# Convolution taps that read the matmul result from PSUM, one tap moved to GpSimd

## The chip, the cores and the metric

The kernel runs on one core of a Trainium2 chip. The metric is device time in microseconds of the whole program, as the median of several executions. Before the change three executions took 3285.49, 3292.46 and 3293.97 us, a median of 3292.46 us. One more execution was recorded by the hardware profiler; the quoted rows come from it.

## The reference, cut to what matters

One layer works on 2048 latent tokens of 1024 channels (a 32 x 64 grid) and 256 context tokens: a mixer (a Fourier branch and a gated recurrence), then a gated MLP with a 3x3 depthwise convolution. The change touches only the MLP:

```python
def conv_ffn(h, w_up, conv_w, conv_b, w_down, rows, cols):
    b, l, _ = h.shape
    z = (h @ w_up).reshape(b, rows, cols, 2 * D_FF)            # 1024 -> 5632 channels
    z = lax.conv_general_dilated(z, conv_w[:, :, None, :], window_strides=(1, 1), padding='SAME',
                                 dimension_numbers=('NHWC', 'HWIO', 'NHWC'),
                                 feature_group_count=2 * D_FF)  # nine taps per channel
    z = z.reshape(b, l, 2 * D_FF) + conv_b
    return (jax.nn.silu(z[..., :D_FF]) * z[..., D_FF:]) @ w_down
```

All data is float32. Channels lie on the 128 partitions, so 5632 channels are 44 tiles of 128 channels x 2048 tokens, and the convolution of a tile is nine shifted multiply-adds with one weight per partition.

## The kernel before, in words

Every large product is made of three matmuls on operands that are split into a high part (a cast on ScalarE, line 102) and a remainder (a subtraction, line 103, on GpSimd unless VectorE is named). Phases 1 and 2 make the mixer's output and the normed input h2 of the MLP. They stay as they are.

`phase3` loops over 22 channel pairs j, and for each over two halves: half 0 is the channel tile that goes through silu, half 1 the one that multiplies it. I count the 44 tiles in the order of work, t = 2j + half. For a tile, 96 matmuls (4 blocks of 512 tokens x 8 x 3, lines 144 to 146) fill `z`, four PSUM banks. There are two such buffers, `za` for half 0 and `zb` for half 1, so TensorE fills one while the other is emptied. ScalarE then copies `z` to SBUF (`zs`, line 952, two buffers), makes the centre tap with the bias (`ac`, line 953, three buffers), and VectorE adds the eight other taps from `zs` (line 979). After half 1, `gate` takes silu of the first half on ScalarE (963), multiplies the halves on GpSimd (964) and stores the product to DRAM (`dZ`, 965). The weights `w_up` of a tile have two buffers, so those of tile t+2 are loaded, cast and subtracted once tile t's matmuls are through.

`down` multiplies the stored product with `ffn_down` in eight groups of 22 k-steps, 12 matmuls each (lines 1020 to 1022), into four banks `dn`, two sets in turn. Its first group (gi = 0) loads the weights `wd` too, subtracts most of them on VectorE, and its PSUM pool comes after both `z` buffers are released. Its last input, the product of the last pair, is made by `last()` in the middle of that group.

Each engine works through its own queue in order; the layer that records the program orders each queue, and an instruction that waits holds all that stand behind it on that engine. DMAs are issued from the queue of SyncE.

Of the kernel before, what the change touches and what calls it, by code (L numbers as in the profile page):

```python
# [17 lines left out]
F32 = mybir.dt.float32  # L18
# [8 lines left out]
P = 128  # L27
# [3 lines left out]
NB = 4            # 512-token blocks  # L31
TB = 512
KD = D // P       # 8
DFF = 2816
NF = DFF // P     # 22
# [10 lines left out]
def constants():  # L46
    """Arrays that depend on the shapes alone."""
    n2 = np.arange(128)
    # level masks: entry (s, t) belongs to the level whose block size first separates s and t
# [5 lines left out]
    cmask = np.stack(lev, 1)                       # [s, 8, t]  # L55
    # twiddled 128-point transforms, one table for each residue k1
# [13 lines left out]
    ch = np.stack([np.cos(ang), np.sin(ang)], 1) / 512.0             # [c, 2, c']  # L70
    eye = np.eye(128)
    rst = np.zeros((128, 640))
    rst[:, 127::128] = 1.0                                           # where the scans restart
# [5 lines left out]
def fap(t, off, dims):  # L79
    """Access pattern over the free elements of a whole tile."""  # L80
    a = t[:]
    return bass.AP(a.tensor, a.offset + off, [list(a.ap[0])] + [list(q) for q in dims])


class Banks:
    """PSUM tiles from the pool that holds their tag."""
# [8 lines left out]
class Layer:  # L95
# [3 lines left out]
    # ------------------------------------------------------------------ helpers  # L99
    def split(self, hi, lo, raw, eng=None):  # L100
        """hi = raw rounded to 12 bits, lo = raw - hi."""
        self.nc.scalar.copy(hi, raw)  # L102
        (eng or self.nc.gpsimd).tensor_tensor(lo, raw, hi, op=SUB)  # L103

    def load_split(self, hi, lo, src, eng=None, pool=None, bufs=2):
        """Load [128, n] or [128, k, c] float32 data of at most 512 columns and split it."""
# [10 lines left out]
    def rsqrt(self, pool, v, n):  # L117
        """v ** -0.5 for positive v of shape [128, n]: bit-level guess and three Newton steps."""
# [11 lines left out]
    def load_w(self, ap, name):  # L130
        """A [1024, 128] column tile of a weight matrix -> hi, lo tiles [128, 8, 128]."""
# [8 lines left out]
    def mm3(self, ps, pairs, start=True, stop=True):  # L140
        """Accumulate the products of the (lhs_hi, lhs_lo, rhs_hi, rhs_lo) in pairs."""
# [7 lines left out]
    # ------------------------------------------------------------------ the layer  # L149
# [44 lines left out]
    # ------------------------------------------------------------------ phase 1  # L194
    def phase1(self):
# [6 lines left out]
        self.mod_A = pc.tile([P, KD], F32, name="mod_A")       # norm1_g * (1 + scale)  # L202
# [17 lines left out]
        # the projections fill TensorE between the small products of the two branches  # L220
# [21 lines left out]
    def drain(self):  # L242
        """Trace the rest of the filler's first part and go on to the next."""
        for _ in self.filler.pop(0):
            pass

    def project_all(self, h):
        """The projections of head h for the state passes; from the second head on, with parts of the
        later modulations."""
# [8 lines left out]
    def vec_rows(self, p0):  # L258
        """Small vectors, loaded as rows of 128 and turned into columns."""
# [17 lines left out]
    def startup(self, p0):  # L277
        nc, a = self.nc, self.a
        ps = self.ps
        # silu(c), silu(c_ctx) as columns  # L280
# [7 lines left out]
        # weights of the FNet channels; one half sits where the context goes later  # L288
# [9 lines left out]

        # shift and scale of the first sub-layer, for latents and context: silu(c)^T @ ada_w; the last
        # 512 columns by VectorE, the others by TensorE  # L300
# [45 lines left out]
        # token tiles -> modulated, transposed, split; the products of a block follow the transposes of  # L346
        # the next one
# [24 lines left out]
        # softmax over the two rows of hg_lb, first row  # L372
# [14 lines left out]
        # conv taps as columns  # L387
# [10 lines left out]
    def load_x(self, p0, blk):  # L398
        """The token tiles of a block, each token scaled to unit mean square."""
# [19 lines left out]
    def modulate_steps(self, pool, xs, A, B, hi, lo, tags, every):  # L419
        """[tok, d] tiles -> transposed h = x * A[d] + B[d], split into hi and lo [d, 8, tok]."""  # L420
# [23 lines left out]
    def fill(self, n):  # L444
        """Trace up to n steps of the projections that wait in self.filler; a context in which
        TensorE's instructions are queued behind them."""
# [5 lines left out]
    def project_steps(self, kind, h):  # L452
        """One 128-channel tile of x @ w_in (channel-major), with its activation, to DRAM, in steps
        of three products."""
# [29 lines left out]
    # ------------------------------------------------------------------ FNet branch  # L484
# [9 lines left out]
    def fnet(self, p1, g):  # L494
        nc, a, ps = self.nc, self.a, self.ps
        X = p1.tile([P, 2, TB], F32, name="fX", tag="fX")           # blocks 0, 1 (later G0, G2)
# [436 lines left out]
    def phase3(self, p5):  # L933
        tc, nc, a = self.tc, self.nc, self.a
        with ExitStack() as es:
            es.push(self.psA.__exit__)
            for j in range(NF):
# [19 lines left out]
                if j < NF - 1:  # L957
                    last()
# [119 lines left out]
```

## Time and profile before

| | us |
|---|---|
| median of three executions | 3292.46 |
| lowest, highest | 3285.49, 3293.97 |
| span of the profiled execution | 3293.7 |
| TensorE busy in it | 3128.3 (95%) |
| VectorE busy | 2007.5 (61%) |
| ScalarE busy | 933.0 (28%) |
| GpSimd busy | 957.0 (29%) |

The profiled execution lies 1.2 us over the median of the others, so sums can be made against its span. In the rows, PE is TensorE, DVE VectorE, ACT ScalarE, POOL GpSimd and SP SyncE; "L979" is line 979. Busy time of TensorE is the sum of pipelined matmuls that overlap: one lasts 0.39 us and the next starts after some 0.23 us. Whether TensorE is held up is therefore read from the starts of matmuls and from their number in a stretch of time, not from its busy share.

### The profile page before, as it was taken

Reading aid. Unit: us, or ns where it says so; the run is one execution under the profiler, and the core shown is the slowest. Engines: PE = TensorE matmul, PEld = TensorE weight load, DVE = VectorE, ACT = ScalarE, POOL = GpSimd, SP = SyncE. Lnnn points to the kernel's source line nnn. Section 1 sums busy time; section 2 is a strip of 40 time slices with the busy share of each in tenths; the row PEclk is TensorE's granted clock in tenths of the full one; section 3 lists DMA queues with packets and bytes.
Section 4 is the critical chain, followed back from the end, with each engine's and each line's share of the span. In section 5 each row is a group of like instructions: output and inputs, shape, how many; then the busy total and the mean of one; then the engine's idle time right before and its main releaser. Section 6 shows DMA issues by size and latency. Waiting matters only on the chain.

```text
span 3293.7 us, 38879 instructions
## 1 busy us (share of the span) xinstructions
PE 3128.3 (95%) x14955; PEld 2576.7 (78%) x14955; DVE 2007.5 (61%) x2538; ACT 933.0 (28%) x1498; POOL 957.0 (29%) x514
## 2 busy tenths in 40 slices
PE   7999999999999999999999999999999997999998
PEld 4977788888888888777778777777777776788886
DVE  5355543576666611566458988988988999302324
ACT  3322112233333321333232222222122122323322
POOL 2200110000000011345333434334343343544443
PEclk8999999999999999999999999999999998999999
DMA  6255654423323234555531111101111112534643
GB/s 223 85 166 182 196 166 138 134 95 102 106 90 105 86 111 145 187 165 183 178 110 36 58 36 52 48 32 51 45 36 48 45 46 72 192 121 155 220 147 131
DMA packets 278506, 372.59 MB, mean 113 GB/s; under 512 B 20253, under 2 KB 154289, under 8 KB 274993
## 3 DMA queue, kind: packets, MB, share of 16 engines
q1 hardware_dynamic: 278321, 370.11, 34.3%
q8 instruction: 118, 1.93, 0.2%
q14 instruction: 67, 0.55, 0.1%
HBM read 268.58 MB, written 101.45 MB: 112 GB/s over the span
## 4 chain that ended last, share of the span: by engine, by line
PE 49%; DVE 31%; DMA 8%; issue 5%; ACT 3%; POOL 3%; SPq 0%; ACTq 0%; DVEq 0%; POOLq 0%
DVE ac L979 27%; PE pj L145 8%; PE pj L144 8%; PE pj L146 8%; PE dn L1022 4%; PE dn L1020 4%; PE dn L1021 4%; PE pa L773 3%; ACT ac L953 1%; DMA rw<-in_w_out_dram 1%; DMA rw<-in_w_b_dram 1%; POOL wab L103 1%; PE wo L906 1%; PE wo L908 1%; PE wo L907 1%
## 5 line engine op out<-in xcount | busy, mean ns | idle before, releaser
L979 DVE SCALAR_TENSOR_TENSOR ac<-zs,cw,ac 128x1953 f32<-128x1953 f32 (+2 forms) x352 | 970.2, 2761 | 105.9 <-ACT ac L953 95.3
L146 PE MATMUL z<-h,w_up 128*128 128x512 f32 x1408 | 565.3, 402 | 58.4 <-POOL w_up L103 58.4
L144 PE MATMUL z<-h,w_up 128*128 128x512 f32 x1408 | 560.9, 398 | 1.9 <-DVE mt L912 1.9
L145 PE MATMUL z<-h,w_up 128*128 128x512 f32 x1408 | 560.2, 398 | 0.0
L146 PEld LDWEIGHTS z<-h,w_up 128*128 128x128 f32 x1408 | 272.1, 193 | 126.1 <-POOL w_up L103 69.3
L103 POOL TENSOR_TENSOR w_up<-rw,w_up 128x512 fp32r<-128x512 f32 x88 | 267.5, 3058 | 348.6 <-ACT w_up L102 348.5
L103 POOL TENSOR_TENSOR gl<-rw,gh 128x512 fp32r<-128x512 f32 x176 | 244.4, 1391 | 272.3 <-ACT gh L102 266.0
L144 PEld LDWEIGHTS z<-h,w_up 128*128 128x128 f32 x1408 | 272.6, 194 | 59.2 <-issue 2.3
L145 PEld LDWEIGHTS z<-h,w_up 128*128 128x128 f32 x1408 | 272.0, 193 | 58.4
L1020 PE MATMUL dn<-wd,gh 128*128 128x512 f32 x704 | 278.7, 396 | 22.0 <-ACT zs L952 20.9
L1022 PE MATMUL dn<-wd,gl 128*128 128x512 f32 x704 | 278.9, 396 | 4.0 <-POOL gl L103 4.0
L1021 PE MATMUL dn<-wd,gh 128*128 128x512 f32 x704 | 278.1, 395 | 0.0
L964 POOL TENSOR_TENSOR ac<-ac 128x2048 f32<-128x2048 f32 x21 | 138.8, 6609 | 274.8 <-DVE ac L979 274.8
L102 ACT CAST gh<-rw 128x512 fp32r<-128x512 f32 x176 | 109.1, 621 | 350.9 <-PE dn L1021 219.4
L952 ACT COPY zs<-z 128x2048 f32<-128x2048 f32 x44 | 82.3, 1872 | 392.2 <-PE z L146 392.2
L479 ACT ACTIVATE ev<-pj 128x512 f32<-128x512 f32 (+1 forms) x136 | 79.8, 587 | 354.0 <-PE pj L146 326.3
L1020 PEld LDWEIGHTS dn<-wd,gh 128*128 128x128 f32 x704 | 133.1, 189 | 54.0 <-ACT zs L952 21.3
L1038 DVE TENSOR_TENSOR dtmp<-dn,m 128x512 f32<-128x512 f32 x32 | 21.6, 685 | 247.2 <-PE dn L1022 247.1
L1022 PEld LDWEIGHTS dn<-wd,gl 128*128 128x128 f32 x704 | 133.0, 189 | 38.2 <-POOL gl L103 7.7
L1021 PEld LDWEIGHTS dn<-wd,gh 128*128 128x128 f32 x704 | 133.0, 189 | 30.5
L773 PEld LDWEIGHTS pa<-bQ,bkc 128*128 128x128 f32 x896 | 120.7, 191 | 16.8 <-issue 10.4
L773 PE MATMUL pa<-bQ,bkc 128*128 128x128 f32 x896 | 127.5, 286 | 1.2
(303 smaller groups left out, 6105.8 us busy)
## 6 DMA issues: line engine op xcount, KB each, us to landing
rw<-dZ SPq DMA_DIRECT2D x176, 256.0 KB, 3.1
rw<-in_ffn_up_dram SPq DMA_DIRECT2D x88, 256.0 KB, 3.0
dZ<-ac SPq DMA_DIRECT2D x22, 1024.0 KB, 3.9
rw<-in_w_in_dram SPq DMA_DIRECT2D x80, 256.0 KB, 3.2
maw<-in_ada_w_dram SPq DMA_DIRECT2D x64, 256.0 KB, 3.2
rw<-in_w_out_dram SPq DMA_DIRECT2D x64, 256.0 KB, 2.7
x<-dX SPq DMA_DIRECT2D x48, 256.0 KB, 5.3
rw<-in_ffn_down_dram SPq DMA_DIRECT2D x44, 256.0 KB, 3.1
```

The lines of the kernel that those rows point to most:

```text
L102: self.nc.scalar.copy(hi, raw)
L103: (eng or self.nc.gpsimd).tensor_tensor(lo, raw, hi, op=SUB)
L144: self.nc.tensor.matmul(ps, lh, rh, start=start and i == 0, stop=False)
L145: self.nc.tensor.matmul(ps, lh, rl, start=False, stop=False)
L146: mm = self.nc.tensor.matmul(ps, ll, rh, start=False, stop=stop and i == last)
L773: mm = nc.tensor.matmul(pa[:, c], kc[:, c], fap(Q, w * P, [(2 * m, nw), (W + m, 2), (1, m)]), start=True, stop=True)
L952: nc.scalar.copy(zs, z)
L964: (nc.gpsimd if j < NF - 1 else nc.vector).tensor_tensor(acc[0], acc[0], acc[1], op=MUL)
L979: nc.vector.scalar_tensor_tensor(o, z3[:, r0 + dy:r1 + dy, c0 + dx:c1 + dx], self.cw[:, k, jj:jj + 1], o, op0=MUL, op1=ADD)
L1020: nc.tensor.matmul(accs[i], gh[:, t], wh, start=(kk == 0), stop=False)
L1021: nc.tensor.matmul(accs[i], gh[:, t], wl, start=False, stop=False)
L1022: nc.tensor.matmul(accs[i], gl[:, t], wh, start=False, stop=(kk == NF - 1))
```

## The change

The copy `zs` is gone. ScalarE reads `z` from PSUM twice: for the centre tap `ac`, and for `be`, z times the weight of the tap one row below (tap 7: row +1, column 0). VectorE adds the seven other taps straight from PSUM. GpSimd then adds `be`, shifted by one row of 64, to `ac`. silu of the first half moves ahead of the second half's convolution. The buffers `za` and `zb` stay open into `down`, whose first two groups accumulate in them; and in the first group the remainders of the first eight `wd` tiles are made on GpSimd. (Comments and docstrings are dropped in the new file, which moves no instruction.)

```diff
 def phase3(self, p5):
...
-                    zs = p5.tile([P, SEQ], F32, name="zs", tag="zs", bufs=2)
-                    nc.scalar.copy(zs, z)
-                    nc.scalar.activation(ac, zs, AF.Identity, scale=self.cw[:, 4, jj:jj + 1], bias=self.v("cb", jj))
-                    self.conv(ac, zs, jj)
+                nc.scalar.activation(ac, z, AF.Identity, scale=self.cw[:, 4, jj:jj + 1], bias=self.v("cb", jj))
+                be = p5.tile([P, SEQ], F32, name="be", tag="be", bufs=2)
+                nc.scalar.activation(be, z, AF.Copy, scale=self.cw[:, 7, jj:jj + 1])
+                if half:
+                    nc.scalar.activation(acc[0], acc[0], AF.Silu)
+                self.conv(ac, z, jj)
+                nc.gpsimd.tensor_tensor(ac[:, :SEQ - 64], ac[:, :SEQ - 64], be[:, 64:], op=ADD)
...
 def gate(self, j, acc):
-        nc.scalar.activation(acc[0], acc[0], AF.Silu)
         (nc.gpsimd if j < NF - 1 else nc.vector).tensor_tensor(acc[0], acc[0], acc[1], op=MUL)
         nc.sync.dma_start(self.dZ[j], acc[0])
...
 def conv(self, ac, z, jj):
-                if dy == 0 and dx == 0:
+                if dx == 0 and dy >= 0:
                     continue
...
 def down(self, last, pools):
-                accs = [ps.tile([P, TB], F32, name=f"dn{i}", tag=f"dn{i}_{gi % 2}") for i in range(4)]
+                if gi < 2:
+                    dn = (self.zb if gi else self.za).tile([P, SEQ], F32, name="dn", tag="z")
+                    accs = [dn[:, i * TB:(i + 1) * TB] for i in range(4)]
+                else:
+                    if gi < 4:
+                        (self.psB if gi % 2 else self.psA).__exit__(None, None, None)
+                        ps.append(es.enter_context(tc.tile_pool(name=f"ps3{gi}", bufs=1, reuse_waits="tile", space=PSUM,
+                                                                side="left" if gi % 2 else "right")))
+                    accs = [ps[gi % 2].tile([P, TB], F32, name=f"dn{i}", tag=f"dn{i}") for i in range(4)]
...
-                                        None if gi == 0 and k in (0, 2, 4) else nc.vector, *((self.pw, 2) if gi == 0 else (p6, 4)))
+                                        None if gi == 0 and k < 8 else nc.vector, *((self.pw, 2) if gi == 0 else (p6, 4)))
```

The recording layer moves instructions with it. First place: ScalarE's queue in the middle of phase 3, one pair of tiles. Before (`w_up_...` are the casts of one tile's weights):

```order
L952 COPY zs<-z 128x2048
L102 CAST w_up_16136<-rw 128x512
L953 ACTIVATE ac<-zs,vt,cw 128x2048
L102 CAST w_up_16136<-rw 128x512
L952 COPY zs<-z 128x2048
L963 ACTIVATE ac<-ac 128x2048
L953 ACTIVATE ac<-zs,vt,cw 128x2048
L102 CAST w_up_16254<-rw 128x512 x2
```

and now:

```order
L953 ACTIVATE ac<-z,vt,cw 128x2048
L955 ACTIVATE be<-z,cw 128x2048
L102 CAST w_up_16136<-rw 128x512 x2
L953 ACTIVATE ac<-z,vt,cw 128x2048
L955 ACTIVATE be<-z,cw 128x2048
L957 ACTIVATE ac<-ac 128x2048
L102 CAST w_up_16254<-rw 128x512 x2
```

Before, the silu of a finished pair (L963) stood ahead of the next centre tap (L953), which the next tile's taps need. Now silu (L957) stands behind both reads of `z`. The first tap of a tile waits for both of these reads, since all three read the same banks.

Second place: GpSimd's queue at the same pair. Before (L964 is the gate's product):

```order
L964 TENSOR_TENSOR ac<-ac 128x2048
L103 TENSOR_TENSOR w_up_16136<-rw,w_up_16136 128x512 x2
L103 TENSOR_TENSOR w_up_16254<-rw,w_up_16254 128x512 x2
L964 TENSOR_TENSOR ac<-ac 128x2048
L103 TENSOR_TENSOR w_up_16375<-rw,w_up_16375 128x512 x2
```

and now:

```order
L968 TENSOR_TENSOR ac<-ac 128x2048
L103 TENSOR_TENSOR w_up_16136<-rw,w_up_16136 128x512 x2
L959 TENSOR_TENSOR ac<-ac,be 128x1984
L103 TENSOR_TENSOR w_up_16254<-rw,w_up_16254 128x512 x2
L959 TENSOR_TENSOR ac<-ac,be 128x1984
L968 TENSOR_TENSOR ac<-ac 128x2048
L103 TENSOR_TENSOR w_up_16375<-rw,w_up_16375 128x512 x2
```

Each tile has one addition more (L959), which waits for the tile's seventh tap and holds up the remainders of the weights behind it.

Third place: ScalarE's queue where phase 3 gives way to `down`. Before:

```order
L952 COPY zs<-z 128x2048
L953 ACTIVATE ac<-zs,vt,cw 128x2048
L102 CAST wd_19488<-rw 128x512 x4
L102 CAST wd_19577<-rw 128x512 x3
L952 COPY zs<-z 128x2048
L102 CAST wd_19577<-rw 128x512
L953 ACTIVATE ac<-zs,vt,cw 128x2048
L102 CAST wd_19666<-rw 128x512
L102 CAST gh<-rw 128x512
L963 ACTIVATE ac<-ac 128x2048
```

and now:

```order
L953 ACTIVATE ac<-z,vt,cw 128x2048
L955 ACTIVATE be<-z,cw 128x2048
L102 CAST wd_19481<-rw 128x512 x4
L102 CAST wd_19570<-rw 128x512 x4
L102 CAST wd_19659<-rw 128x512 x2
L953 ACTIVATE ac<-z,vt,cw 128x2048
L955 ACTIVATE be<-z,cw 128x2048
L957 ACTIVATE ac<-ac 128x2048
L102 CAST gh<-rw 128x512 x2
```

Ten casts of `wd` now stand ahead of the last tile's centre tap (seven before the last copy `zs` until now), and the casts of `gh` for the k-steps from the fourth on (three are made early in phase 3) stand behind the last tile's two reads and the silu.

More of the change, by code (lines that the diff above doesn't have):

```diff
@@ L934, in phase3 @@
         tc, nc, a = self.tc, self.nc, self.a
-        with ExitStack() as es:
-            es.push(self.psA.__exit__)
-            for j in range(NF):
-                acc = []
-                for half in range(2):
-                    jj = j + half * NF
-                    wh, wl = self.load_w(a["ffn_up"][0, :, jj * P:(jj + 1) * P], f"up{jj}")
-                    if jj == NF:
-                        self.psB.__exit__(None, None, None)
-                        zb = es.enter_context(tc.tile_pool(name="ps2b", bufs=1, reuse_waits="tile", space=PSUM))
-                    z = (zb if half else self.za).tile([P, SEQ], F32, name="z", tag="z")
-                    ac = p5.tile([P, SEQ], F32, name="ac", tag="ac", bufs=3)
-                    for n in range(NB):
-                        hh, hl = self.h2[n]
-                        self.mm3(z[:, n * TB:(n + 1) * TB],
-                                 [(wh[:, k, :], wl[:, k, :], hh[:, k, :], hl[:, k, :]) for k in range(KD)])
-                    zs = p5.tile([P, SEQ], F32, name="zs", tag="zs", bufs=2)
-                    nc.scalar.copy(zs, z)
-                    nc.scalar.activation(ac, zs, AF.Identity, scale=self.cw[:, 4, jj:jj + 1], bias=self.v("cb", jj))
-                    self.conv(ac, zs, jj)
-                    acc.append(ac)
-                last = lambda: self.gate(j, acc)
-                if j < NF - 1:
-                    last()
@@ new lines, in phase3 @@
+        for j in range(NF):
+            acc = []
+            for half in range(2):
+                jj = j + half * NF
+                wh, wl = self.load_w(a["ffn_up"][0, :, jj * P:(jj + 1) * P], f"up{jj}")
+                if jj == NF:
+                    self.psB.__exit__(None, None, None)
+                    self.psB = tc.tile_pool(name="ps2b", bufs=1, reuse_waits="tile", space=PSUM)
+                    self.zb = self.psB.__enter__()
+                z = (self.zb if half else self.za).tile([P, SEQ], F32, name="z", tag="z")
+                ac = p5.tile([P, SEQ], F32, name="ac", tag="ac", bufs=3)
+                for n in range(NB):
+                    hh, hl = self.h2[n]
+                    self.mm3(z[:, n * TB:(n + 1) * TB],
+                             [(wh[:, k, :], wl[:, k, :], hh[:, k, :], hl[:, k, :]) for k in range(KD)])
+                nc.scalar.activation(ac, z, AF.Identity, scale=self.cw[:, 4, jj:jj + 1], bias=self.v("cb", jj))
[5 more added lines that the diff above has]
+                nc.gpsimd.tensor_tensor(ac[:, :SEQ - 64], ac[:, :SEQ - 64], be[:, 64:], op=ADD)
+                acc.append(ac)
+            last = lambda: self.gate(j, acc)
+            if j < NF - 1:
+                last()
@@ L983, in down @@
         tc, nc, a, pr = self.tc, self.nc, self.a, self.pr
-        with tc.tile_pool(name="ps3", bufs=1, reuse_waits="tile", space=PSUM) as ps:
+        with ExitStack() as es:
+            ps = []
             for gi in range(2 * NB):
```

## The prediction

> **What bounds the kernel now.** I read the page first. Its chain of waits names an engine that is 61% busy overall, and its costliest group names the line:
>
> ```profile
> PE 49%; DVE 31%; DMA 8%; issue 5%; ACT 3%; POOL 3%; SPq 0%; ACTq 0%; DVEq 0%; POOLq 0%
> L979 DVE SCALAR_TENSOR_TENSOR ac<-zs,cw,ac 128x1953 f32<-128x1953 f32 (+2 forms) x352 | 970.2, 2761 | 105.9 <-ACT ac L953 95.3
> ```
>
> The taps fill phase 3. Busy time per stage (us, then busy time with count per engine) shows where TensorE is fed and where not:
>
> ```profile
> 1727.00:1836.00 109.00, 109.00 (x482) 90.28 (x481) 93.26 (x35) 30.21 (x24) 40.73 (x12) 1.00 0.11 38
> 1836.00:2760.00 924.00, 865.61 (x3650) 705.00 (x3650) 838.01 (x304) 225.56 (x173) 366.03 (x97) 0.96 0.13 44
> ```
>
> In the first five tiles 482 matmuls take 109 us, 0.226 each; later 3650 take 924 us, 0.253 each. So something else sets the pace. The timeline of one pair of tiles, VectorE, ScalarE, GpSimd (start, duration, idle before and what ended it):
>
> ```profile
> 2344.42 44.64 DVE L979 SCALAR_TENSOR_TENSOR ac<-zs,cw,ac 128x2016 f32<-128x2016 f32 x16 [4.03 <-ACT ac L953]
> 2393.09 8.82 DVE L979 SCALAR_TENSOR_TENSOR ac<-zs,cw,ac 128x2016 f32<-128x2016 f32 x3 [4.03 <-ACT ac L953]
> ...
> 2389.15 1.92 ACT L963 ACTIVATE ac<-ac 128x2048 f32<-128x2048 f32 x1 [17.16 <-DVE ac L979]
> 2390.97 2.08 ACT L953 ACTIVATE ac<-zs,vt,cw 128x2048 f32<-128x2048 f32 x1
> ...
> 2364.78 6.60 POOL L964 TENSOR_TENSOR ac<-ac 128x2048 f32<-128x2048 f32 x1 [13.63 <-DVE ac L979]
> ```
>
> A pair takes 2393.09 - 2344.42 = 48.67 us: 16 taps, 44.64, then 4.03 in which VectorE waits for silu and the centre tap, queued behind its own last tap. That closed loop is the bound; TensorE needs less:
>
> ```profile
> 2344.99 0.39 PE L146 MATMUL z<-h,w_up 128*128 128x512 f32 x1
> 2347.71 0.39 PE L146 MATMUL z<-h,w_up 128*128 128x512 f32 x1
> 2348.13 1.88 ACT L952 COPY zs<-z 128x2048 f32<-128x2048 f32 x1 [2.72 <-PE z L146]
> ```
>
> Twelve starts in 2.72 us are 0.2267 each, a tile of 96 is 21.76 us, a pair 43.52. The loop costs 5.15 us a pair over that.
>
> **Why a tap costs 2.79.** Minimum, median and maximum of VectorE groups, with one row of the chain:
>
> ```profile
> L979 DVE SCALAR_TENSOR_TENSOR ac<-zs,cw,ac x352: 2240/2285/6549, 1732.3 to 2812.1; 128x1953 f32<-128x1953 f32 x88, 128x2016 f32<-128x2016 f32 x44, 128x1984 f32<-128x1984 f32 x44
> 2366.97 6.54 DVE ac L979
> L606 DVE SCALAR_TENSOR_TENSOR macc<-maw,sc,macc x56: 724/751/1851, 309.0 to 525.0; 128x512 f32<-128x512 f32 x56
> L824 DVE SCALAR_TENSOR_TENSOR bg<-pt,vt,bg x16: 729/730/752, 655.1 to 1169.5; 128x512 f32<-128x512 f32 x16
> L1039 DVE TENSOR_TENSOR x<-x,dtmp x32: 674/682/1808, 2851.1 to 3282.3; 128x512 f32<-128x512 f32 x32
> L1038 DVE TENSOR_TENSOR dtmp<-dn,m x32: 673/684/693, 2849.8 to 3281.4; 128x512 f32<-128x512 f32 x32
> L879 DVE TENSOR_TENSOR gt<-pj,gt x64: 675/682/694, 1301.2 to 1599.0; 128x512 f32<-128x512 f32 x64
> ```
>
> The 6.54 us tap overlaps the 6.60 us GpSimd product: with both tensors in SBUF (L979, L606, L1039) an instruction can be held while GpSimd runs, up to 2.9 times its minimum. With one input in PSUM (L824, L1038, L879) no maximum is over 1.04 times the minimum, in 112 instructions. L824 has the form of the new taps (PSUM, weight, SBUF) and L606 that of the old ones; at 512 columns they take 730 and 751.
>
> **The change, part by part.** *Taps.* I take a new one at the old median, 2.29: seven make 16.0 us. Bounds: below, the minimum, 2.24 each, 15.7; above, L824 in proportion to length, 0.730 x 1953/512 = 2.78, 19.5.
>
> *ScalarE.* The copy goes, one scaled read comes. The two reads of `z`:
>
> ```profile
> L952 ACT COPY zs<-z x44: 1860/1873/1880, 1727.9 to 2779.6; 128x2048 f32<-128x2048 f32 x44
> L953 ACT ACTIVATE ac<-zs,vt,cw x42: 2079/2091/2108, 1754.9 to 2740.8; 128x2048 f32<-128x2048 f32 x42
> ```
>
> From PSUM I take L952's 1.87 for each (2.09, the centre tap's own row, as the other bound). silu is no longer in the way.
>
> *The new hold.* `z` now stays occupied until its seventh tap. From the tile's last matmul start: 0.42 to ScalarE's start (2347.71 to 2348.13), 2 x 1.87 for the reads, 16.0 for the taps, some 0.2 for handovers: 20.4. The other buffer's matmuls give 21.76 + 0.23 = 22.0. So TensorE isn't held, by 1.6 us a tile, 0.23 a tap. This margin is what the forecast hangs on: with C for a tile's taps, a pair takes the larger of 43.52 and 25.8 + C (two reads and handovers, 4.3, less the 0.23, plus 21.76, plus C), so C decides from 17.7 on.
>
> [...]
>
> *GpSimd.* One addition a tile. Its size class:
>
> ```profile
> L103 POOL TENSOR_TENSOR gl<-rw,gh x176: 1272/1297/3311, 1792.9 to 3270.7; 128x512 fp32r<-128x512 f32 x176
> L964 POOL TENSOR_TENSOR ac<-ac x21: 6592/6611/6622, 1778.3 to 2754.4; 128x2048 f32<-128x2048 f32 x21
> ```
>
> Between 4 x 1.3 = 5.2 undisturbed and 6.6. After a pair's second tile, counted from its last matmul: taps end at 20.4, addition 25.6 to 27, product 30.8 to 33.6, then two weight subtractions queued behind (2.6 to 6.5): 33.4 to 40.1, needed at 43.7. Hidden, by 3.6 us at worst.
>
> *Sum for phase 3.* TensorE then runs at 21.76 a tile. The first copy starts at 1727.9; 43 tiles later is 2663.6. Now the last z matmul starts at 2760.21, so a copy could start at 2760.6. Saved: 97.0.
>
> *The passage to `down`.* Rows of TensorE, ScalarE and the weights' casts:
>
> ```profile
> 2760.21 0.39 PE L146 MATMUL z<-h,w_up 128*128 128x512 f32 x1
> 2781.48 0.80 PE L1020 MATMUL dn<-wd,gh 128*128 128x512 f32 x1 [20.88 <-ACT zs L952]
> 2851.69 0.39 PE L1020 MATMUL dn<-wd,gh 128*128 128x512 f32 x1
> ...
> 2773.06 1.29 ACT L102 CAST wd<-rw 128x512 fp32r<-128x512 f32 x2 [4.72 <-DMA rw<-in_ffn_down_dram]
> 2779.04 0.62 ACT L102 CAST wd<-rw 128x512 fp32r<-128x512 f32 x1 [4.69 <-DMA rw<-in_ffn_down_dram]
> 2779.57 1.86 ACT L952 COPY zs<-z 128x2048 f32<-128x2048 f32 x1
> ...
> 2767.56 2.81 POOL L103 TENSOR_TENSOR wd<-rw,wd 128x512 fp32r<-128x512 f32 x1 [3.34 <-ACT wd L102]
> ```
>
> TensorE waits 20.88 us for the last copy, itself late behind casts and taps; the first group then runs 2781.48 to 2851.69, 70.2 us. Now its accumulators are `za`, free 20.4 us after the tile before the last, so before z ends: 21.0 saved. But the casts that make the inputs late are late still. Ten `wd` casts stand ahead of the last centre tap. They come two per round, 6.0 us now (2773.06 to 2779.04) with subtractions of 2.8, some 4.5 when these take 1.3; four rounds after GpSimd is free of the last product (8.7 us into the last tile) put the tenth about 5 us past the last z matmul. Two reads, silu, a cast and a subtraction later, at 13, comes the fourth k-step's input, wanted at 0.23 + 3 x 12 x 0.2267 = 8.4 (the first three are made early in phase 3). That is a stall of some 5 us plus a slow restart; with it I leave the first group at 70 us (a clean one would take 61, one with two such stalls 78).
>
> The rest of that group keeps up:
>
> ```profile
> 2760.00:2852.00 92.00, 65.94 (x269) 50.41 (x268) 64.76 (x39) 31.13 (x46) 44.49 (x25) 0.89 0.51 166
> 2779.69 0.69 DVE L103 TENSOR_TENSOR wd<-rw,wd 128x512 fp32r<-128x512 f32 x1 [0.47 <-ACT wd L102]
> 2790.09 1.77 DVE L103 TENSOR_TENSOR wd<-rw,wd 128x512 fp32r<-128x512 f32 x1
> L1022 PE MATMUL dn<-wd,gl x704: 387/393/632, 2782.5 to 3280.9; 128*128 128x512 f32 x176
> ```
>
> The granted clock there is 0.89 against 1.00 while TensorE is fed, which is the slow restart. VectorE starts the last tile's taps about 9 us after z ends and has seven `wd` subtractions among them, 0.69 to 1.77 each: done at 30 to 38. GpSimd's addition (5 to 7), VectorE's product (2.3), the store and the load of it follow; that is 45 to 55, and the last k-step wants it at 13 + 18 x 2.72 = 62. The other seven groups take (3280.9 - 2851.69)/7 = 61.3 each, and nothing in them changes, though they take their banks from other pools.
>
> The total: 3293.7 - 97.0 - 21.0 = 3175.7 of span, 1.2 over the median as before; I say 3175.
>
> **Rivals.** *(a) PSUM taps dearer.* If a tap goes by proportion (2.78), C is 19.7 with handovers and a pair 45.5, 2.0 over TensorE's, times 21: 3217. For: 2000-column reads across four banks occur only on ScalarE (L952). [...]
>
> *(b) GpSimd holds taps in PSUM too, in part.* The first tile's addition falls mostly on ScalarE's reads; the product (4.25 extra, 6.54 less 2.29) and the weights' subtractions stay on taps:
>
> ```profile
> 2346.77 3.24 DVE ac L979
> 2345.02 6.12 POOL L103 TENSOR_TENSOR w_up<-rw,w_up 128x512 fp32r<-128x512 f32 x2 [15.87 <-ACT w_up L102]
> ```
>
> Two subtractions lengthen two taps by 0.95 each (3.24 less 2.29). With 16.1 undisturbed, C is 18.0 in one tile and 22.2 in the other, a pair 45.9, 3225.
>
> *(c) Slower: both additions of a pair land on taps as well and hold them like the product does.* C becomes (32.2 + 3 x 4.25 + 4 x 0.95)/2 = 24.4, a pair 50.2, 1.5 more than now: 21 x 6.7 over the forecast, 3316. It decides from C = 23.9, 3.4 us a tap, counting the saving at the passage. Against (b) and (c) stand the flat maxima of L1038 and L879, and a place where both kinds run under a busy GpSimd:
>
> ```profile
> 2850.18 8.21 POOL L103 TENSOR_TENSOR gl<-rw,gh 128x512 fp32r<-128x512 f32 x5 [0.97 <-ACT gh L102]
> 2851.12 2.62 DVE L1039 TENSOR_TENSOR x<-x,dtmp 128x512 f32<-128x512 f32 x2
> 2853.66 1.27 DVE L1038 TENSOR_TENSOR dtmp<-dn,m 128x512 f32<-128x512 f32 x2
> ```
>
> Two with both inputs in SBUF take 2.62 us, twice their normal time; two with one in PSUM take 1.27, their normal time. For them speaks only that this is one place, at a quarter of a tap's length.
>
> *(d) The bound isn't the loop:* phase 3 keeps its pace for a reason not seen, and only the passage gains: 3272.
>
> **How the numbers follow.** Forecast 80%, (a) 7%, (b) 6%, (c) 4%, (d) 3%. The forecast's own range is 3158 (a clean first group, 9 less, and 8 of spread between executions, as before) to 3198 (a bad first group, 8 more, and C up to 18.4, 0.7 x 21 = 15 more). The range to name is 3158 to 3218: it reaches to (a). Below 3158 there is no room, since TensorE would have to beat 21.76 a tile; with ScalarE's reads at 2.09 instead of 1.87 nothing moves, as the hold stays under 22.0. This kernel tells apart 0.3%, 10 us: faster 0.94, same 0.02, slower 0.04.
>
> **What would show it.** Right: z matmuls 0.227 us apart throughout, no wait of theirs on VectorE or GpSimd, taps near 2.3 with a maximum under 2.5, GpSimd's 128x512 subtractions near 1.3 and its product near 5.2 in phase 3. Wrong: taps of 2.8 with z matmuls waiting for L983 (a); taps of 6 us beside GpSimd (b, c); a wait of over 10 us at the first `dn` matmuls (the passage).

## The result, and the profile after

| | median us | ratio to before, 95% interval |
|---|---|---|
| before | 3289.59 (3285.49 to 3293.97, 4 runs) | |
| after | 3175.29 (3174.20 to 3181.74, 4 runs) | 0.9656, 0.9641 to 0.9671 |
| after, second series on another occasion | 3183.03 (3178.69 to 3187.55, 4 runs) | 0.9672, 0.9654 to 0.9691 |

The first series is the one that the prediction is held against: 3175 forecast, 3175.29 measured. The second shows that the agreement to a third of a microsecond is luck, as the stages will tell. The profiled execution of after has a span of 3173.2 us.

The page of after, its chain by engine and its costliest groups (busy us, mean ns, then idle time before and what ended it):

```profile
PE 77%; DMA 6%; DVE 5%; POOL 2%; issue 2%; ACT 2%; SPq 0%; DVEq 0%; ACTq 0%; POOLq 0%
L983 DVE SCALAR_TENSOR_TENSOR ac<-z,cw,ac 128x1953 f32<-128x1953 f32 (+2 forms) x308 | 700.8, 2275 | 255.4 <-ACT be L955 244.1
L144 PE MATMUL z<-h,w_up 128*128 128x512 f32 x1408 | 548.0, 389 | 1.9 <-ACT w_up L102 1.9
L959 POOL TENSOR_TENSOR ac<-ac,be 128x1984 f32<-128x1984 f32 x44 | 196.7, 4471 | 427.6 <-DVE ac L983 427.6
```

TensorE's share of the chain went from 49% to 77% and VectorE's from 31% to 5%. The taps now cost 700.8 us instead of 970.2, and VectorE is idle for 255.4 us in front of them: it waits for ScalarE's reads of a fresh `z`. Before, VectorE's loop held TensorE by way of GpSimd: the only wait of TensorE that the profile lists from 1836 to 2760 us of before is

```profile
PE z L146 <- POOL w_up L103: 58.4, 23, 4.1
```

(us in total, times, longest). These are the remainders of the weights. They stand behind the product L964 in GpSimd's queue, and that product waits for the last tap of its pair. In after this wait is gone. The stages (us, then busy time with count for PE, PEld, DVE, ACT, POOL, then the granted clock, DMA share, GB/s):

```profile
1718.00:1827.00 109.00, 109.00 (x483) 90.28 (x482) 79.64 (x35) 30.98 (x25) 43.61 (x19) 1.00 0.16 49
1827.00:2654.00 827.00, 827.00 (x3650) 685.03 (x3649) 605.30 (x266) 225.47 (x176) 359.19 (x138) 1.00 0.16 51
2654.00:2732.00 78.00, 66.29 (x270) 51.73 (x269) 36.74 (x23) 28.40 (x42) 42.70 (x27) 0.93 0.53 172
```

The same 3650 matmuls that took 924 us take 827.00, all of it busy, at a granted clock of 1.00 (0.96 before). After the first tile no gap is left in phase 3. One pair of tiles of after, on VectorE, ScalarE and GpSimd (start, duration, idle before and what ended it):

```profile
2310.27 16.14 DVE L983 SCALAR_TENSOR_TENSOR ac<-z,cw,ac 128x2016 f32<-128x2016 f32 x7 [5.80 <-ACT be L955]
2331.85 16.14 DVE L983 SCALAR_TENSOR_TENSOR ac<-z,cw,ac 128x2016 f32<-128x2016 f32 x7 [5.43 <-ACT be L955]
...
2306.26 2.06 ACT L953 ACTIVATE ac<-z,vt,cw 128x2048 f32<-128x2048 f32 x1 [16.94 <-PE z L146]
2308.23 1.96 ACT L955 ACTIVATE be<-z,cw 128x2048 f32<-128x2048 f32 x1
2310.08 1.91 ACT L957 ACTIVATE ac<-ac 128x2048 f32<-128x2048 f32 x1
...
2326.56 4.47 POOL L959 TENSOR_TENSOR ac<-ac,be 128x1984 f32<-128x1984 f32 x1 [11.45 <-DVE ac L983]
2331.11 4.63 POOL L968 TENSOR_TENSOR ac<-ac 128x2048 f32<-128x2048 f32 x1
2335.70 2.54 POOL L103 TENSOR_TENSOR w_up<-rw,w_up 128x512 fp32r<-128x512 f32 x2
```

silu (L957) now runs beside the first taps instead of in front of the centre tap. GpSimd's product and two subtractions (2331.11 to 2338.24) lie beside taps but for their first 0.7 us, and the taps take the same 16.14 us as those of the tile before. The rows by which the prediction wanted to be judged (minimum, median and maximum ns):

```profile
L983 DVE SCALAR_TENSOR_TENSOR ac<-z,cw,ac x308: 2240/2253/2320, 1722.6 to 2684.8; 128x1953 f32<-128x1953 f32 x88, 128x2016 f32<-128x2016 f32 x44, 128x1984 f32<-128x1984 f32 x22
L103 POOL TENSOR_TENSOR w_up<-rw,w_up x88: 1269/1297/1750, 1683.7 to 2618.5; 128x512 fp32r<-128x512 f32 x88
L968 POOL TENSOR_TENSOR ac<-ac x21: 4623/4630/4642, 1765.1 to 2635.8; 128x2048 f32<-128x2048 f32 x21
L953 ACT ACTIVATE ac<-z,vt,cw x44: 2052/2067/2067, 1718.6 to 2662.2; 128x2048 f32<-128x2048 f32 x44
L955 ACT ACTIVATE be<-z,cw x44: 1957/1962/1968, 1720.6 to 2664.2; 128x2048 f32<-128x2048 f32 x44
```

Taps: maximum 2.32 (6.55 before). Subtractions: median 1.30. Product: 4.63 (6.61 before). The reads of `z`: 2.07 and 1.96.

To say where the time went, I cut every profiled execution of this study at the same three points: the first and the last start of a `z` matmul, and the first matmul of `down`'s second group. The columns are the start of `z`, the time from there to the last `z` matmul, from that to the second group, and the rest.

| kernel | start of z | z stage | last z to second group | rest | span |
|---|---|---|---|---|---|
| before | 1699.0 | 1061.2 | 91.5 | 442.0 | 3293.7 |
| after | 1690.2 | 963.7 | 77.3 | 442.0 | 3173.2 |
| after, second series | 1702.1 | 963.7 | 77.2 | 442.0 | 3185.0 |

The change takes 97.5 us from the `z` stage (0.4 of them in its first tile) and 14.2 from the passage, 111.7 together. Nothing of the program ahead of `z` was changed, and its first column still moves: by 12 us between two executions of the same kernel, and between 1690.2 and 1703.6 over the eleven profiles here. The first profile of after happened to be the earliest of them. So 8.8 of the 120.5 us between the two spans are no work of the change.

### The profile page after: what moved, and what is told of

Same layout as the page of the kernel before. It is cut to its first block, busy times and chain, and to the rows that moved or that the text cites. A ratio compares the mean times of both kernels' runs of the same rounds, so it can differ in the third digit from the quotient of the medians.

```text
span 3173.2 us, 38929 instructions
## 1 busy us (share of the span) xinstructions
PE 3086.0 (97%) x14955; PEld 2554.0 (80%) x14955; DVE 1735.2 (55%) x2489; ACT 930.4 (29%) x1498; POOL 947.3 (30%) x563
## 4 chain that ended last, share of the span: by engine, by line
PE 77%; DMA 6%; DVE 5%; POOL 2%; issue 2%; ACT 2%; SPq 0%; DVEq 0%; ACTq 0%; POOLq 0%
PE z L146 9%; PE z L145 9%; PE z L144 9%; PE pj L146 8%; PE pj L144 8%; PE pj L145 8%; PE dn L1035 5%; PE dn L1033 5%; PE dn L1034 5%; PE pa L773 4%; DMA rw<-in_w_b_dram 1%; PE kv L645 1%; PE wo L906 1%; PE wo L908 1%; PE wo L907 1%
## 5 line engine op out<-in xcount | busy, mean ns | idle before, releaser
L983 DVE SCALAR_TENSOR_TENSOR ac<-z,cw,ac 128x1953 f32<-128x1953 f32 (+2 forms) x308 | 700.8, 2275 | 255.4 <-ACT be L955 244.1
L144 PE MATMUL z<-h,w_up 128*128 128x512 f32 x1408 | 548.0, 389 | 1.9 <-ACT w_up L102 1.9
L146 PE MATMUL z<-h,w_up 128*128 128x512 f32 x1408 | 548.0, 389 | 0.0
L145 PE MATMUL z<-h,w_up 128*128 128x512 f32 x1408 | 548.0, 389 | 0.0
L959 POOL TENSOR_TENSOR ac<-ac,be 128x1984 f32<-128x1984 f32 x44 | 196.7, 4471 | 427.6 <-DVE ac L983 427.6
L103 POOL TENSOR_TENSOR gl<-rw,gh 128x512 fp32r<-128x512 f32 x176 | 233.0, 1326 | 271.7 <-ACT gh L102 262.2
L144 PEld LDWEIGHTS z<-h,w_up 128*128 128x128 f32 x1408 | 264.4, 188 | 57.0 <-ACT w_up L102 2.3
L145 PEld LDWEIGHTS z<-h,w_up 128*128 128x128 f32 x1408 | 264.4, 188 | 54.8
L146 PEld LDWEIGHTS z<-h,w_up 128*128 128x128 f32 x1408 | 264.4, 188 | 54.5
L953 ACT ACTIVATE ac<-z,vt,cw 128x2048 f32<-128x2048 f32 x44 | 90.9, 2066 | 639.0 <-PE z L146 639.0
L479 ACT ACTIVATE ev<-pj 128x512 f32<-128x512 f32 (+1 forms) x136 | 79.6, 586 | 358.3 <-PE pj L146 336.9
L103 POOL TENSOR_TENSOR w_up<-rw,w_up 128x512 fp32r<-128x512 f32 x88 | 112.8, 1306 | 92.0 <-ACT w_up L102 92.0
```

Of the source, the lines that this page charges most:

```text
L144: self.nc.tensor.matmul(ps, lh, rh, start=start and i == 0, stop=False)
L145: self.nc.tensor.matmul(ps, lh, rl, start=False, stop=False)
L146: mm = self.nc.tensor.matmul(ps, ll, rh, start=False, stop=stop and i == last)
L953: nc.scalar.activation(ac, z, AF.Identity, scale=self.cw[:, 4, jj:jj + 1], bias=self.v("cb", jj))
L959: nc.gpsimd.tensor_tensor(ac[:, :SEQ - 64], ac[:, :SEQ - 64], be[:, 64:], op=ADD)
L983: nc.vector.scalar_tensor_tensor(o, z3[:, r0 + dy:r1 + dy, c0 + dx:c1 + dx], self.cw[:, k, jj:jj + 1], o, op0=MUL, op1=ADD)
```

## The experiments

The medians beside the stages; "before" on the same chips had medians between 3289.27 and 3291.74. The rows of before and after are above.

| kernel | median us | ratio, 95% interval | start of z | z stage | last z to second group | rest |
|---|---|---|---|---|---|---|
| e1_silu_place | 3291.61 | 1.0000, 0.9991 to 1.0009 | 1694.9 | 1060.3 | 90.9 | 442.0 |
| e1b_silu_behind | 3210.65 | 0.9763, 0.9745 to 0.9781 | 1703.6 | 978.4 | 90.1 | 443.7 |
| e2_eight_psum | 3176.88 | 0.9653, 0.9639 to 0.9667 | 1695.1 | 965.9 | 69.1 | 444.0 |
| e4_hold | 3209.34 | 0.9751, 0.9735 to 0.9767 | 1693.6 | 990.8 | 82.7 | 443.1 |
| e5b_silu_ahead | 3240.26 | 0.9849, 0.9833 to 0.9865 | 1697.3 | 1020.9 | 79.6 | 445.1 |
| e6_old_banks | 3200.03 | 0.9730, 0.9715 to 0.9744 | 1691.6 | 964.2 | 99.3 | 442.0 |
| b4_centre_first | 3174.04 | 0.9651, 0.9637 to 0.9666 | 1696.6 | 965.8 | 66.7 | 446.1 |
| b6_second_group | 3165.95 | 0.9621, 0.9607 to 0.9636 | 1693.5 | 965.7 | 60.1 | 444.2 |

### e1 and e1b: is the loop the bound?

The theory: VectorE's taps and the 4.03 us in which it waits for silu and the centre tap form a closed loop. The rival: that gap is only where lost time shows. The first try moved silu in the program's text:

```diff
                     nc.scalar.activation(ac, zs, AF.Identity, scale=..., bias=...)
+                    if half:
+                        nc.scalar.activation(acc[0], acc[0], AF.Silu)
                     self.conv(ac, zs, jj)
@@ gate
-        nc.scalar.activation(acc[0], acc[0], AF.Silu)
```

> The kernel before with one line moved: silu of a pair's first half is written behind the second half's centre tap instead of in front of the product; the copy zs, its eight taps on VectorE and everything else stay. Theory (closed loop of VectorE's taps and the 4.03 us in which it waits for silu and the centre tap): the 4.03 us gap goes, a pair falls from 48.67 us to VectorE's own 44.6 to 44.9, so some 19 pairs give back 4 us each: 75 to 83 us, 3207 to 3217 us, with the passage to down as before (20 us of wait at the first dn matmul). Taps stay at a mean near 2.79 and a maximum near 6.5, since the product of GpSimd still holds one of them. Rival (the gain of the change needs taps that GpSimd doesn't hold, and the gap is only where the lost time shows): pairs stay at 48 to 49 us and the time within 10 us of 3290.

Nothing changed: ratio 1.0000. That would have spoken for the rival, had the trace not shown that the experiment had not taken place. ScalarE's rows of e1 (line 955 is the moved silu, 953 the centre tap):

```profile
2366.23 1.87 ACT L952 COPY zs<-z 128x2048 f32<-128x2048 f32 x1 [16.20 <-PE z L146]
2384.45 1.92 ACT L955 ACTIVATE ac<-ac 128x2048 f32<-128x2048 f32 x1 [16.35 <-DVE ac L980]
2386.27 2.08 ACT L953 ACTIVATE ac<-zs,vt,cw 128x2048 f32<-128x2048 f32 x1
```

silu still stands in front. The order on an engine comes from the program's scheduler, not from the order of the lines. e1b ties it:

```diff
-                    nc.scalar.activation(ac, zs, AF.Identity, scale=..., bias=...)
+                    centre = nc.scalar.activation(ac, zs, AF.Identity, scale=..., bias=...)
+                    if half:
+                        with tc.issue_after(centre.ins):
+                            nc.scalar.activation(acc[0], acc[0], AF.Silu)
```

> The kernel before with silu of a pair's first half tied behind the second half's centre tap on ScalarE (in e1_silu_place the line had moved, but ScalarE's rows were still copy, silu, centre tap). Copy zs, eight taps from SBUF, GpSimd's work: unchanged. Theory (closed loop): the 4.03 us gap goes, since the centre tap can run as soon as zs is there, 15 us earlier; a pair is then VectorE's 44.6 to 44.9; (1032.7 - 935.7) of phase 3 falls to 20 to 28, so 70 to 77 us are saved: 3212 to 3220. The passage stays as before. Rival (taps that GpSimd holds fill whatever VectorE is given, or something else sets 48.67): 3280 to 3295.

ScalarE and VectorE of e1b (953 the centre tap, 956 silu, 981 the taps):

```profile
2370.11 1.87 ACT L952 COPY zs<-z 128x2048 f32<-128x2048 f32 x1 [16.86 <-PE z L146]
2374.29 2.10 ACT L953 ACTIVATE ac<-zs,vt,cw 128x2048 f32<-128x2048 f32 x1
2386.18 1.92 ACT L956 ACTIVATE ac<-ac 128x2048 f32<-128x2048 f32 x1 [9.79 <-DVE ac L981]
...
2358.55 93.70 DVE L981 SCALAR_TENSOR_TENSOR ac<-zs,cw,ac 128x1953 f32<-128x1953 f32 x34
```

In e1 the centre tap, behind the waiting silu, starts 18.17 us after its copy's end; here, ahead of silu, 2.31 us after it. It is done 10 us before VectorE needs it, and VectorE runs 34 taps in a row without a gap. A pair takes 44.6 us, as expected; the time is 3210.65, 1 under the expected 3212 to 3220. So the theory holds, and it says something about the change: the place of one instruction alone, with the copy, the SBUF taps and GpSimd's work as before, brings 82.8 us in the `z` stage, where the whole change brings 97.5. That makes it a sufficient step, not a necessary one, as e2 will show. The taps of e1b are as long as those of before:

```profile
L981 DVE SCALAR_TENSOR_TENSOR ac<-zs,cw,ac x352: 2239/2286/6551, 1736.4 to 2731.5; 128x1953 f32<-128x1953 f32 x88, 128x2016 f32<-128x2016 f32 x44, 128x1984 f32<-128x1984 f32 x44
L103 POOL TENSOR_TENSOR w_up<-rw,w_up x88: 1272/3198/3308, 1697.1 to 2656.4; 128x512 fp32r<-128x512 f32 x88
```

### e2: is the tap for GpSimd needed?

```diff
-                be = p5.tile(...)
-                nc.scalar.activation(be, z, AF.Copy, scale=self.cw[:, 7, jj:jj + 1])
-                nc.gpsimd.tensor_tensor(ac[:, :SEQ - 64], ac[:, :SEQ - 64], be[:, 64:], op=ADD)
@@ conv
-                if dx == 0 and dy >= 0:
+                if dx == 0 and dy == 0:
```

> The changed kernel with the moved tap taken back: VectorE adds eight taps from PSUM, be and GpSimd's addition are gone. Theory (TensorE bound as long as z is held for less than 22.0 us): the hold is 0.42 + 2.07 for the centre tap + 8 x 2.29 + 0.2 = 21.0, one us under the limit, so z matmuls stay 21.76 us a tile and phase 3 is 935.7 us as in the changed kernel; all in all 3165 to 3180 (the passage has no GpSimd addition of 4.5 us in it, so its second stall of 4.6 us may go). Rival (the tap for GpSimd is needed to stay under TensorE's time): z matmuls wait for VectorE, pairs of 44 to 46 us, 3185 to 3225.

The `z` stage is 965.9 us, 2.2 more than with seven taps, 1.0 of it a single wait (line 980 is the tap):

```profile
PE dn L1032 <- POOL gl L103: 4.6, 7, 1.0
PE z L144 <- DVE ac L980: 1.0, 1, 1.0
PE dn L1030 <- ACT gh L102: 0.2, 1, 0.2
...
L980 DVE SCALAR_TENSOR_TENSOR ac<-z,cw,ac x352: 2239/2264/2320, 1726.0 to 2690.8; 128x1953 f32<-128x1953 f32 x88, 128x2016 f32<-128x2016 f32 x44, 128x1984 f32<-128x1984 f32 x44
L103 POOL TENSOR_TENSOR w_up<-rw,w_up x88: 1274/1297/1655, 1688.8 to 2622.5; 128x512 fp32r<-128x512 f32 x88
```

With the second read of `z` gone, the taps start 2.5 to 3.2 us after the last `z` matmul instead of 4.4 to 4.6, and the eighth tap fits.

The edit also moved an instruction that it does not name. In e2 silu (line 955) stands ahead of the second half's centre tap (953) again, in every pair, as it did before the change:

```profile
2311.96 1.92 ACT L955 ACTIVATE ac<-ac 128x2048 f32<-128x2048 f32 x1 [17.57 <-DVE ac L980]
2313.78 2.04 ACT L953 ACTIVATE ac<-z,vt,cw 128x2048 f32<-128x2048 f32 x1
```

It costs next to nothing here: silu waits for VectorE's last tap alone, the hold is 21.7 us in the second halves instead of 21.0, which is still under 22.0 (the first pair is an exception: 23.0, and there stands the one wait). Beside the kernel before, with silu ahead in both, the `z` stage is 95.3 us shorter (1061.2 to 965.9). So there are two ways out of the loop, silu behind the centre tap (82.8 us, e1b) and taps from PSUM (95.3 us), and they do not add up.

The passage is 8.2 us shorter than in after (69.1 against 77.3). By the stages e2 is 4.0 us better than the changed kernel (-8.2 + 2.2 + 2.0 in the rest); the medians, 3176.88 against 3175.29 and 3183.03, cannot tell them apart. So giving one tap to GpSimd is a part of the change that brings nothing to be measured.

Beside e1b, this kernel shows what dropping the copy and reading PSUM is worth once the loop's gap is gone: 12.5 us of `z` stage (978.4 to 965.9, although silu stands ahead in e2 and behind in e1b), besides the early start of `down` that goes with it. The shortest tap takes 2239 ns in both. What differs is the maximum, 6551 against 2320, and GpSimd's subtraction, median 3198 against 1297. The profiles of before and after have the same difference: in before 162 of the 352 taps overlap an instruction of GpSimd and take up to 6.55 us, and the 190 others stay within 2.32 us; of the 308 taps of after 140 overlap one, and all 308 stay within 2.32 us. The taps of 1953 columns with no instruction of GpSimd beside them take 2252 ns in the median in before (148 taps) and in after (166). A more direct test, e3_sbuf_taps (the changed kernel with centre tap, scaled copy and seven taps read from an SBUF copy of `z`), has no time: its tiles need 48 kb per partition where 40.5 kb are left.

### e4: is the hold of z really the limit?

```diff
-                nc.scalar.activation(be, z, AF.Copy, scale=self.cw[:, 7, jj:jj + 1])
+                nc.scalar.activation(be, z, AF.Copy, scale=self.nil)
@@ conv
-                if dx == 0 and dy >= 0:
+                if dx == 0 and dy == 0:
```

`nil` is a column of zeros.

> The changed kernel with all eight taps on VectorE and the scaled copy and GpSimd's addition kept, the scale being zero, so that a zero is added: the result is the same, and z is held one tap longer. Theory (z's hold decides, limit 22.0): the hold grows from 20.5 to 20.7 by a tap of 2.29 to 22.8 to 23.0, so TensorE waits 0.8 to 1.0 us a pair, 17 to 22 us over phase 3: 3192 to 3200, and z matmuls now wait for VectorE (first time in this series). Rival (the margin isn't what the sum says; VectorE, at 55% busy, has room for an eighth tap): 3170 to 3180 with pairs of 43.52.

TensorE in e4, waits from 1745 us to the end of phase 3 (us in total, times, longest), and one of them in the timeline:

```profile
PE z L144 <- DVE ac L985: 19.9, 24, 1.0
...
2302.90 0.39 PE L146 MATMUL z<-h,w_up 128*128 128x512 f32 x1
2304.33 0.47 PE L144 MATMUL z<-h,w_up 128*128 128x512 f32 x1 [1.04 <-DVE ac L985]
```

Both kernels make the same two reads; one more tap of 2.3 us on VectorE, and TensorE waits for it. The mechanism is as forecast, the size is not: pairs of 44.81 us, 1.29 over 43.52, where the formula gave 0.8 to 1.0. It left out the 0.15 us between the last tap's end (2304.18) and the first matmul, and 0.1 of slower first matmuls. The `z` stage grew by 27.1 us and the passage by 5.4; 3209.34 against the 3192 to 3200 that I expected. VectorE is busy for 55% of the whole program of after and for 73% of phase 3 (605.30 of 827.00 us), and still there is no room for one more tap: what counts is when in the tile it ends.

### e5b: does the place of silu matter with PSUM taps too?

```diff
-                nc.scalar.activation(ac, z, AF.Identity, scale=..., bias=...)
+                if half:
+                    silu = nc.scalar.activation(acc[0], acc[0], AF.Silu)
+                with tc.issue_after(silu.ins) if half else nullcontext():
+                    nc.scalar.activation(ac, z, AF.Identity, scale=..., bias=...)
@@ after the second read
-                if half:
-                    nc.scalar.activation(acc[0], acc[0], AF.Silu)
```

> The changed kernel with silu of a pair's first half tied in front of the second half's centre tap, as it stood before; taps and banks as in the changed kernel. Theory (z is held until its last tap, limit 22.0 us): silu waits for GpSimd's addition, 20.7 + 0.2 + 4.5 = 25.3 us after the first half's z; it ends at 27.2, the second half's reads at 31.3; that z is released late and TensorE waits x a pair. With x, the second half's z itself comes x later, so x = 22.7 + (26.8 - 21.76 - x) - 22.0 up to rounding, 2x = 4 to 6: pairs of 45.5 to 46.5, 41 to 63 us more than 3175: 3216 to 3238. Rival (once the taps read PSUM the place of silu no longer matters): 3172 to 3180.

ScalarE (954 silu, 956 and 958 the two reads) and TensorE's waits over phase 3:

```profile
2303.99 1.92 ACT L954 ACTIVATE ac<-ac 128x2048 f32<-128x2048 f32 x1 [2.25 <-POOL ac L960]
2305.81 2.04 ACT L956 ACTIVATE ac<-z,vt,cw 128x2048 f32<-128x2048 f32 x1
...
PE z L144 <- DVE ac L984: 35.5, 12, 3.3
```

silu waits for GpSimd's addition, the reads of `z` wait for silu, and TensorE for the late taps: 26.9 us in place of 21.76 for every fourth tile, 92.2 us for two pairs, 46.1 a pair (expected 45.5 to 46.5). The `z` stage is 57.2 us longer, the whole kernel 3240.26, 2 over my range. The place matters because of what silu waits for: here it is GpSimd's addition, in e2 VectorE's last tap. There silu stands ahead too (without addition and second read), and the `z` stage is only 2.2 us longer than in after. With silu left in its place, the change would have brought 49 us (3289.27 less 3240.26), less than half of its gain.

### e6: what is the early start of down worth?

```diff
-                if gi < 2:
-                    dn = (self.zb if gi else self.za).tile([P, SEQ], F32, name="dn", tag="z")
-                    accs = [dn[:, i * TB:(i + 1) * TB] for i in range(4)]
-                else: ...
+                if gi == 0:
+                    self.psB.__exit__(None, None, None)
+                    self.psA.__exit__(None, None, None)
+                    ps = es.enter_context(tc.tile_pool(name="ps3", bufs=1, ..., space=PSUM))
+                accs = [ps.tile([P, TB], F32, name=f"dn{i}", tag=f"dn{i}_{gi % 2}") for i in range(4)]
```

> The changed kernel with the accumulators of down in one PSUM pool opened after both z buffers are closed, as before; phase 3 as in the changed kernel. Theory (the first group's early start is worth what the forecast said): the first dn matmul waits until the last tile's seventh tap, 33 us after the last z matmul instead of 0.2, while casts go on; the first group is then clean, 62 to 66 us instead of 77.1, so it ends 18 to 22 us later: 3193 to 3198. Rival (the group is bound by its inputs, whenever it starts): it ends at the same time, 3172 to 3180.

TensorE's waits from phase 3 to the end of the first group:

```profile
PE dn L1029 <- DVE ac L983: 30.7, 1, 30.7
PE dn L1031 <- POOL gl L103: 4.5, 6, 1.3
```

The first group starts 30.9 us later and takes 68.2 us instead of 77.1: 22.0 us lost, 3200.03 us. I had expected a clean group of 62 to 66 us and 3193 to 3198; its small waits for `gl` remained. So the reuse of the `z` buffers carries its part of the gain.

### b4 and b6: a better passage

With eight PSUM taps the space of `be` is free. b4 puts twice the `gh`/`gl` buffers and landing buffers for the weights there, and ties the `wd` casts from the ninth k-step on behind the last centre tap:

```diff
+                        with tc.issue_after(self.centre.ins) if gi == 0 and k >= 8 else nullcontext():
-                                        ... *((self.pw, 2) if gi == 0 else (p6, 4)))
+                                        ... *((self.p5 if k % 2 else self.pw, 2) if gi == 0 else (p6, 4)))
-                    gp, nb = (pr, 3) if gi == 0 else (p6, 4)
+                    gp, nb = (self.p5 if k % 2 else pr, 3) if gi == 0 else (p6, 4)
```

> e2_eight_psum (eight taps from PSUM, no addition on GpSimd) with the space of the scaled copy used for down's first group: twice the gh and gl buffers, and four instead of two landing buffers for its weights; the weights' casts from the ninth k-step on are tied behind the last centre tap. Theory (the first group lost 7.5 us in e2_eight_psum and 15.8 in the changed kernel over its clean 61.35, to inputs that are late): first group 62 to 66 us, phase 3 at 935.7 to 938, 3160 to 3172. Rival (first group held by the stores and loads of z themselves, or the extra loads in flight collide): first group 68 us or more, 3172 to 3182.

All 22 steps of the first group now run at 2.72 us, 59.8 in all. But the time stayed at 3174.04, the rival's range: the wait had moved to the first step of the second group.

```profile
PE dn L1032 <- ACT gh L102: 6.4, 1, 6.4
PE z L144 <- DVE ac L981: 1.0, 1, 1.0
```

Its landing buffers lie in the space that the first group's new buffers hold until its last matmul. b6 lets the first three steps of the second group use the old buffers:

```diff
-                    gp, nb = (self.p5 if k % 2 else pr, 3) if gi == 0 else (p6, 4)
+                    gp, nb = (self.p5 if k % 2 else pr, 3) if gi == 0 else (pr, 3) if gi == 1 and k < 3 else (p6, 4)
```

> b4_centre_first, in which the wait of 6.8 us stood at the second group's first k-step (its landing buffers lie in the space that the first group's extra buffers hold until its last matmul); now the second group's first three k-steps use the old gh and gl buffers, which are free earlier. Theory (only the place of the wait keeps b4_centre_first at 3174): first group 60 us, second 61 to 63 instead of 6.8 + 64.6, so 8 to 9 us less than b4_centre_first: 3163 to 3170. Rival (a late input moves on to the next k-step once more, or the loads collide): 3171 to 3178.

> The changed kernel as it is, beside b6_second_group on the same chip, to see how far its phases before the change vary: phase 3 935.7 us, first group 77.1, as in its first profile; the start of z within 1690 to 1705; 3170 to 3182.

b6, TensorE's waits over the same stretch:

```profile
PE z L144 <- DVE ac L981: 1.0, 1, 1.0
PE dn L1035 <- POOL gl L103: 0.6, 1, 0.6
```

3165.95 us (3165.32 to 3167.59), beside 3183.03 for the changed kernel on the same chip, which is 1 over the range named for it. Of the 17.1 us between the medians 12.9 are b6's own by the stages: 17.1 at the passage, less 2.0 in the `z` stage and 2.2 in the rest; where the 2.2 come from was not followed up. It is the fastest kernel of this study, and silu stands ahead of the centre tap in it as in e2.

## Why the prediction was right, and where it was off

**What bounds the kernel: right.** e1b removed the wait and nothing else, and the pair fell from 48.67 to 44.6 us. One detail ahead of the prediction was told wrongly: silu is not that of a finished pair. In the trace it runs right behind the taps of the pair's first half and ahead of the second half's centre tap. The arithmetic of the loop used the right rows.

**Taps: right, and for the reason given.** C was put at 16.0 and measured 16.14. The rows L824 and L1038, which I took as evidence that a PSUM input escapes GpSimd, carried over to instructions four times as long. Rivals (a), (b) and (c) needed longer taps and fell with the maximum of 2.32. One slip changed nothing: rival (a) counts the 0.2 us of handovers twice, 4 us of its 3217.

**Hold: right, with a margin up to a fifth smaller.** I took 1.87 for each read of `z`; they took 2.07 and 1.96. The last tap ends 20.5 to 20.7 us after the tile's last matmul start, so 1.3 to 1.5 us of the 22.0 were left, not 1.6. e4 used them up and TensorE waited.

**Phase 3: right.** 97.0 forecast from the end of the first tile on, 97.5 measured with the first tile and 97.1 without: every tile but the first takes 21.76 us. Rival (d) fell.

**The passage: mechanism right, size off.** The wait of 20.88 us went, as said: the first `dn` matmul starts 0.23 us after the last `z` matmul. But I left the first group at 70 us and it took 77.1, my "bad" case of two stalls; the term of 21.0 measured 14.2. The first stall came where I put it. The tenth `wd` cast started 7.8 us past the last `z` matmul, not 5, and the fourth input was ready 14.6 us past it, not 13, so the stall cost 6.07 and not 5. TensorE and the casts around it:

```profile
2668.48 0.79 PE L1033 MATMUL dn<-wd,gh 128*128 128x512 f32 x1 [6.07 <-ACT gh L102]
2695.77 0.50 PE L1035 MATMUL dn<-wd,gl 128*128 128x512 f32 x1 [2.69 <-POOL gl L103]
...
2661.68 0.62 ACT L102 CAST wd<-rw 128x512 fp32r<-128x512 f32 x1 [2.00 <-DMA rw<-in_ffn_down_dram]
2662.21 2.05 ACT L953 ACTIVATE ac<-z,vt,cw 128x2048 f32<-128x2048 f32 x1
...
2689.59 4.44 POOL L959 TENSOR_TENSOR ac<-ac,be 128x1984 f32<-128x1984 f32 x1
2693.99 5.00 POOL L103 TENSOR_TENSOR gl<-rw,gh 128x512 fp32r<-128x512 f32 x2
```

The second stall I had not named. I followed the last tile's addition on GpSimd only towards the product that needs it, and not towards the subtractions of `gl` that queue behind it on the same engine: 4.44 us in which no remainder is made. The group lies 17.3 us over 22 steps of 2.72: the first stall and its restart are 8.4 of them, the second 4.6, and four later k-steps of 3.2 to 4.5 us the rest. e2 has neither this addition nor the second read of `z`. Both stalls are gone there, no wait is above 1.0 us, small waits cost 9.0 us of the group in place of 17.3, and its passage is 8.2 us shorter. How much of that is the addition's and how much the read's stays open.

**The total: right partly by luck.** The terms measured 97.5 + 14.2 = 111.7 against 118.0. The missing 6.3 us were made up by a start of `z` that came 8.8 us earlier in the profile of after than in that of before, with the same program ahead of it. Without that the terms give 3292.46 - 111.7 = 3180.8; the second series measured 3183.03.

**GpSimd: right that it is hidden; its product was put at 5.2 to 6.6 and takes 4.63.** From 1.297 us at 512 columns and 4.630 at 2048 I estimate 2.17 ns a column and some 0.19 us that do not grow with the columns; four times the 128x512 duration counts these four times.

The experiments' own expectations failed in three places: e1 (the edit did not reach the engine's order), e4 (27.1 us where 17 to 22 were expected) and b4 (the wait moved by one group). The times of four more missed their ranges by 1 to 2 us: e1b, e5b, e6 and the second series of after.

## What to carry to other kernels

Look for the instruction that stands in front of the critical one in its engine's queue before making anything faster: one silu behind instead of ahead of a centre tap was worth 82.8 us with nothing else changed. It need not be the only way: with shorter taps and no addition on GpSimd the silu could stay ahead (e2). And check the order in the trace after every edit, since moving a line may move nothing (e1), and an edit elsewhere may move what you did not touch (e2).

A buffer that is read by many instructions is released by the last of them (in e4 TensorE waited 24 times, up to 1.0 us, for the last tap of `z`); compare that moment, handovers included, with the time at which the other buffer is full, not the reader's busy share with 100%. When work goes to a third engine, list what queues behind it there at the seams of the program, where that queue is full of other things.

## What the runs showed of the hardware

Behind two waits in after, of 6.07 and 2.69 us, TensorE restarted slowly. The matmuls are 0.227 us apart until 2662.0, and then, from 2668.5 to 2672.1, 0.43 to 0.77; from 2696.4 to 2699.4, behind the shorter wait, they are 0.43 apart. The granted clock (the figure behind the five busy times) in stretches during and behind the two waits:

```profile
2662.00:2668.40 6.40, 0.41 (x2) 0.00 (x0) 4.25 (x3) 6.40 (x6) 1.26 (x1) 0.78 0.24 83
2668.40:2673.00 4.60, 4.38 (x11) 3.04 (x12) 4.57 (x4) 1.78 (x5) 2.52 (x2) 0.57 0.32 101
2692.00:2696.00 4.00, 1.30 (x6) 0.80 (x5) 4.00 (x2) 1.14 (x2) 4.00 (x3) 1.00 0.29 86
2696.00:2700.00 4.00, 4.00 (x12) 3.08 (x12) 4.00 (x3) 1.24 (x2) 3.00 (x2) 0.57 0.69 262
```

It falls to 0.57 behind both waits. A wait of 2.69 us thus made its k-step 7.3 us long instead of 2.72. The 0.96 from 1836 to 2760 us of before, with 23 waits of up to 4.1 us, fits this. Shorter waits of e4 did not bring it about: behind the quoted one of 1.04 us the matmuls are 0.30, 0.24 and 0.23 us apart and then 0.227, and the granted clock over the whole execution is 0.992, beside 0.994 in after.

On ScalarE an activation over 2048 columns of PSUM took 1.87 us as a plain copy, 1.96 with a scale from a column and 2.07 with scale and bias from columns.
